# One read of the prompt heads' keys and queries instead of two, with the second half of the partitions written by the splitting engines

## The chip, the cores and the metric

The kernel runs on one core of a Trainium2 chip. The metric is the device time of one execution in microseconds (us); the time before is the median of three runs, 2407.51 us (2405.63 to 2414.55).

The core's engines each work through their own queue of instructions in order: PE (matrix multiply), DVE (vector), ACT (scalar), POOL (GpSimd), and SP, which here only issues DMA transfers. Sixteen DMA engines move the data.

## What is computed

The reference is one inference step of four layers over a prompt of 1024 tokens and a sample batch of 8 times 4 tokens. The change lies in layer 2, differential attention with 8 heads. Each head has two key halves and two query halves of 64 dimensions, one softmax for each, and one 128-wide value:

```python
q = rope_partial(q.reshape(bsz, t, 2 * N_HEADS, HEAD_DIM), pos) * (HEAD_DIM ** -0.5)
k = rope_partial(k.reshape(bsz, t, 2 * N_HEADS, HEAD_DIM), pos)
...
sc = jnp.einsum('bqhd,bkhd->bhqk', qi, k).astype(jnp.float32)
sc = jnp.where(kpos[None, :] <= qpos[:, None], sc, -jnp.inf)
w = diff_combine(jax.nn.softmax(sc, axis=-1), lam).astype(v.dtype)
return jnp.einsum('bhqk,bkhd->bqhd', w, v)
```

`diff_combine` is p1 - lam * p2 for the two halves of a head. The sample tokens attend to 2048 past positions each, through a paged cache of keys and values (`cache_k`, `cache_v`, 64 MB each).

## The kernel before, in words

Products are made with float32 operands split in two: a rounded high part in the type fp32r, and a low part (the value minus its high part). The projection stage `qkv` writes the rotated prompt keys and queries, transposed, to DRAM (`self.qkT`: 1024 rows of head dimension by 1024 tokens), because they don't fit on chip beside the rest.

`attn_layer` merges generators by costs: `qkv` and `zpath` run together with `sample_keys` (the pages of `cache_k`), then `heads` (the prompt heads) runs together with `sample_values` (the pages of `cache_v`). `self.ahead` is 1.1, so that the values end somewhat before the heads. Within this, the order of instructions on each engine is settled by the framework's planner, from its own estimate of each instruction's time; the heads' work has a raised priority.

`heads` goes through 64 blocks, 8 heads times 8 blocks of 128 queries. A block scores against the keys up to the diagonal (`score`), takes the exponent (`expo`, ACT), joins the two halves (`combine`, DVE), turns the weights (`turn`, PE and ACT), and applies them to the values (`apply`, PE). Scores for half s take one array in which both key parts lie across the partitions: `ks[h]` holds for half s the high part on 64 partitions (`own`) and the low part on the other 64 (`oth`). Queries `qhl` hold high and low part on both halves of the partitions, so that two matmuls over 128 partitions give all four products of the parts.

To fill these, `keys(h, g)` and `queries(h, g)` (g is a half of the tokens) are called 16 times each. `twice` (line 1179) allocates a raw tile and loads it with two transfers of SP (line 1183), each of 64 partitions and each carrying the whole 128 rows. ACT then rounds it (lines 1195 and 1203), and POOL subtracts (lines 1198 and 1204). Calls stand in the block loop: `queries(h, 1)` after block 1, `keys(h + 1, 0)` and `keys(h + 1, 1)` after blocks 4 and 5, `queries(h + 1, 0)` after block 6; the calls of head 0 are made while `zpath` still runs.

Raw tiles are a ring of two, shared with the weight loads of `load_w` (lines 110 to 112); `qhl` lies in a ring of two as well, shared with weights. The value pages come through a ring of five tiles (`vp`, line 1388), issued by SP, and are used by the matmuls `sacc` (line 1524). `cmask` (line 1327), which the first softmax needs, is loaded by SP too.

Of the kernel before, what the change touches and what calls it, by code (L numbers as in the profile page):

```python
# [10 lines left out]
F32 = mybir.dt.float32  # L11
# [4 lines left out]
ALU = mybir.AluOpType  # L16
# [30 lines left out]
class Trunk:  # L47
# [1123 lines left out]
    def heads(self, y):  # L1171
        nc = self.nc
        ident = self.ident
        lo_, hi_ = slice(0, 64), slice(64, 128)
        halves = ((lo_, hi_), (hi_, lo_))
        ks, V, sz, qs, O, ss = {}, {}, {}, {}, {}, {}


        def twice(q, h, g):
            t = self.raw([128, 2, 512], f"tok{q}{h}_{g}")  # L1180
            src = self.qkT[q][128 * h : 128 * h + 128, 512 * g : 512 * g + 512]
            for rows in halves[0]:
                nc.sync.dma_start(t[rows], src.rearrange("(s p) f -> p s f", p=64))
            return t

        def keys(h, g):
            if g == 0:
                ks[h] = self.ppa.tile([128, 2, T], F32R, tag="ks", bufs=self.n_ks, name=f"ks{h}")
                V[h] = self.ppa.tile([128, 8, 128], F32, tag="V", bufs=2, name=f"V{h}")
                nc.sync.dma_start(  # L1190
                    V[h], self.vd[:, 128 * h : 128 * h + 128].rearrange("(j p) f -> p j f", p=128)
                )
            t = twice(1, h, g)
            cs = slice(512 * g, 512 * g + 512)
            nc.scalar.copy(ks[h][:, :, cs], t)
            for s, (own, oth) in enumerate(halves):
                lo = ks[h][oth, s, cs]
                nc.gpsimd.tensor_tensor(lo, t[oth, s], lo.bitcast(F32), ALU.subtract)

        def queries(h, g):  # L1200
            t = twice(0, h, g)
            qhl = self.wtile([128, 2, 2, 512], F32R, f"qhl{h}_{g}")
            nc.scalar.copy(qhl[:, 0], t)
            nc.gpsimd.tensor_tensor(qhl[:, 1], t, qhl.bitcast(F32)[:, 0], ALU.subtract)
            qs[h, g] = qhl

        def product(st, h, qb, s, o, l0, w):
# [108 lines left out]
        def begin(h, qb):  # L1316
            return dict(h=h, qb=qb, S={}, P=[], rr=self.ropep.tile(
                [128, 20], F32, tag="rr", bufs=6, name=f"rr{h}_{qb}"))

        keys(0, 0)  # L1320
        queries(0, 0)
        keys(0, 1)
        yield 0

# [6 lines left out]
        for nxt in blocks[1:] + [None, None, None]:  # L1331
            if old:
                combine(old)
            if cur:
                h, qb = cur["h"], cur["qb"]
                expo(cur, 0)
                score(cur, 1)
                yield 220 * (qb + 1)
                if qb in (2, 5):
                    g = qb // 3  # L1340
                    sz[h, g] = self.pp.tile([128, 512], F32, tag="sz", bufs=self.n_sz, name=f"sz{h}_{g}")
                    nc.sync.dma_start(sz[h, g], self.zd[h][:, 512 * g : 512 * g + 512])
                if qb == 1:
                    queries(h, 1)
                    yield 430
                if h < 7 and qb in (4, 5):
                    keys(h + 1, qb - 4)
                    yield 430
                if h < 7 and qb == 6:
                    queries(h + 1, 0)  # L1350
                    yield 430
# [488 lines left out]
```

## Time and profile before

| what | value |
| --- | --- |
| median of three runs | 2407.51 us |
| profiled execution | 2409.33 us, its span 2407.7 us |
| PE busy over the span | 95% |
| DVE, ACT, POOL busy over the span | 60%, 39%, 14% |
| mean granted PE clock | 0.985 of full speed |
| the stretch in which heads and value pages run together | about 1490 to 1810 us |
| end of the heads | about 1845 us |

Line numbers are those of the kernel before. A row names the engine, the line, the operation, and the tile written and read (out<-in). "PEld" is PE's weight load, which runs beside its matmuls; "SPq" is a DMA being issued on SP. Idle time of an engine is put down to what ended it.

### The profile page before, as it was taken

How to read it: one execution, taken by the hardware profiler on the slowest of the kernel's cores; microseconds unless marked ns; L12 is line 12 of the kernel's file. 1: busy time of each engine (PE TensorE's matmuls, PEld its weight loads, DVE VectorE, ACT ScalarE, POOL GpSimd, SP SyncE). 2: the span in 40 equal slices, each digit the busy share in tenths (PEclk: the TensorE clock that was granted, in tenths of full speed). 3: DMA queues.
4: the chain of work that ended last, by engine and by line, in shares of the span. 5: the costliest groups of instructions: out<-in, count | busy, mean ns of one | idle time of the engine just before them, and what ended most of it. 6: DMA issues, size and time to landing. Idle time of an engine off the chain costs nothing.

```text
span 2407.7 us, 45325 instructions
## 1 busy us (share of the span) xinstructions
PE 2277.3 (95%) x17288; PEld 1946.8 (81%) x17288; DVE 1453.2 (60%) x3015; ACT 929.2 (39%) x1906; POOL 337.1 (14%) x541
## 2 busy tenths in 40 slices
PE   7999999999999999988999998888888999999997
PEld 4989999997888886766666886555557999999997
DVE  6865655457456545656555554677675477666555
ACT  4333333346544423322221113667665243333410
POOL 0200000001001000233223322333220000000000
PEclk9999999999999999999999998999999999999999
DMA  9243344423444535768677766999993222222442
GB/s 329 77 145 111 91 121 150 133 82 120 139 131 124 154 108 171 217 201 255 222 242 253 244 189 203 277 298 291 281 299 116 84 85 62 68 59 70 128 131 76
DMA packets 289391, 393.41 MB, mean 163 GB/s; under 512 B 18749, under 2 KB 197054, under 8 KB 289174
## 3 DMA queue, kind: packets, MB, share of 16 engines
q1 hardware_dynamic: 247190, 306.61, 42.1%
q0 software_dynamic: 20480, 67.13, 9.1%
q10 hardware_dynamic: 21504, 16.78, 2.1%
q8 instruction: 136, 2.23, 0.4%
q14 instruction: 81, 0.66, 0.1%
HBM read 331.14 MB, written 59.31 MB: 162 GB/s over the span
## 4 chain that ended last, share of the span: by engine, by line
PE 64%; issue 13%; DMA 11%; POOLq 5%; POOL 2%; DVE 2%; ACT 1%; SPq 1%; DVEq 0%; ACTq 0%
PE op L127 15%; PE inX L612 12%; PE inZ L612 6%; DMA vp<-cache_v 6%; PE xb L127 4%; PE z L127 4%; POOLq L1381 4%; PE in L127 3%; PE inY L612 3%; PE ada L200 3%; PE in L733 2%; PE in L648 2%; PE g L903 2%; POOL kp L1388 2%; PE sacc L1524 1%
## 5 line engine op out<-in xcount | busy, mean ns | idle before, releaser
L1099 PE MATMUL qk<-wq,ua 128*128 128x512 f32 x1152 | 284.1, 401 | 8.7 <-DVE wq L1067 5.5
L1099 PEld LDWEIGHTS qk<-wq,ua 128*128 128x128 f32 x1152 | 213.2, 189 | 68.4 <-DVE wq L1067 8.1
L1476 DVE STREAM_TRANSPOSE kt<-kp 128x512 f32<-128x512 f32 x256 | 172.0, 697 | 138.5 <-DMA kp<-cache_k 107.1
L1388 POOL DMA_DIRECT2D kp<-cache_k x256 | 137.9, 539 | 336.1 <-DVE kt L1476 188.8
L294 DVE SCALAR_TENSOR_TENSOR r<-op,gate,xr 128x384 f32<-128x384 f32 (+1 forms) x96 | 54.2, 570 | 127.4 <-PE op L127 82.5
L1262 ACT ACTIVATE P<-S,rr 128x512 f32<-128x512 f32 (+2 forms) x192 | 110.8, 583 | 47.1 <-DVE rr L1250 31.5
L1210 PE MATMUL S<-ks,qhl 128*128 128x512 f32 (+2 forms) x384 | 110.8, 395 | 13.8 <-ACT P L1262 7.4
L127 PE MATMUL zz<-ua,wz 128*128 128x384 f32 (+1 forms) x576 | 99.0, 331 | 7.0 <-DVE zt L1165 7.0
L1210 PEld LDWEIGHTS S<-ks,qhl 128*128 128x128 f32 x384 | 60.8, 196 | 54.8 <-ACT P L1262 30.7
L127 PEld LDWEIGHTS zz<-ua,wz 128*128 128x128 f32 x576 | 95.6, 193 | 11.4 <-DVE zt L1165 7.8
L127 PEld LDWEIGHTS z<-ub,wrz 128*128 128x128 f32 x576 | 92.6, 188 | 11.7 <-issue 10.1
L1524 PE MATMUL sacc<-vp,pv 128*16 128x256 f32 x1024 | 80.3, 389 | 22.9 <-DMA vp<-cache_v 22.7
L127 PE MATMUL z<-ub,wrz 128*128 128x384 f32 (+1 forms) x576 | 98.2, 326 | 0.0
L1303 PEld LDWEIGHTS pv<-V,wt 128*128 128x128 f32 x576 | 73.7, 194 | 22.5 <-ACT wt L1295 13.4
L127 PEld LDWEIGHTS xb<-ub,wrx 128*128 128x128 f32 x504 | 80.9, 188 | 12.7 <-issue 9.2
L1420 PE MATMUL sps<-kt,qbd 32*32 32x512 f32 x2048 | 78.8, 621 | 11.9 <-DVE kt L1476 11.9
L331 POOL TENSOR_TENSOR rs<-mv,mhalf 128x1 f32<-128x1 f32 (+1 forms) x36 | 19.1, 541 | 504.3 <-DVE mv L329 497.6
L127 PE MATMUL op<-ua,ub 128*128 128x384 f32 (+1 forms) x504 | 89.7, 333 | 0.0
L127 PEld LDWEIGHTS op<-ua,ub 128*128 128x128 f32 x504 | 81.9, 192 | 9.1 <-issue 9.0
L127 PE MATMUL xb<-ub,wrx 128*128 128x384 f32 (+1 forms) x504 | 87.9, 328 | 0.0
L1303 PE MATMUL pv<-V,wt 128*128 128x128 f32 x576 | 82.3, 284 | 5.8 <-ACT wt L1295 5.3
L200 PE MATMUL ada<-wada,ct 128*32 128x512 f32 x384 | 82.7, 616 | 4.1 <-DMA wada<-w_ada 2.9
(492 smaller groups left out, 5112.4 us busy)
## 6 DMA issues: line engine op xcount, KB each, us to landing
kp<-cache_k POOLq DMA_DIRECT2D x256, 256.0 KB, 3.8
vp<-cache_v SPq DMA_DIRECT2D x128, 512.0 KB, 10.0
wada<-w_ada SPq DMA_DIRECT2D x96, 512.0 KB, 4.2
xa<-xat SPq DMA_DIRECT2D x64, 192.0 KB, 2.6
wra<-a_w_in SPq DMA_DIRECT2D x24, 512.0 KB, 4.1
wrb<-a_w_in SPq DMA_DIRECT2D x24, 512.0 KB, 4.1
xr<-xa SPq DMA_DIRECT2D x64, 192.0 KB, 2.5
tok<-kd SPq DMA_DIRECT2D x32, 256.0 KB, 7.0
```

Source lines behind the costliest of these rows:

```text
L127: nc.tensor.matmul(ps[:, :n], wt[:, wp, k], self.ucols(units[k], up, c), start=i == 0, stop=i == 3 * KB - 1)
L200: nc.tensor.matmul(ps[c : c + 32, :], self.ct[:, k], wts[k // 2][:, k % 2], start=k < 4, stop=k >= 4, tile_position=(0, c),)
L612: nc.tensor.matmul(B[tgt][jj][:, :QH], w[n][:, wp, k], mov[k](jj, up), start=new and m == 0, stop=m == 11, skip_group_check=not new)
L1099: nc.tensor.matmul(ps, u[k][:, c0 : c0 + 128], wq[n, k // 2][:, wp, k % 2], start=i == 0, stop=i == 3 * KB - 1)
L1210: nc.tensor.matmul(st[:, o : o + w], qs[h, g][:, part, s, 128 * qj : 128 * qj + 128], ks[h][:, s, l0 : l0 + w], start=part == 0, stop=part ...
L1262: nc.scalar.activation(p[:, o : o + w], x["S"][s][i][:, :w], AF.Exp, scale=-1.0, bias=rr[:, 6 + s : 7 + s], accum_out=rr[:, c : c + 1])
L1303: nc.tensor.matmul(x["pv"], x["w"][kb // 4][:, j : j + 128], V[h][:, kb], start=kb == 0, stop=kb == qb)
L1381: ld, (r,) = nc.values_load_multi_w_load_instructions(self.ptab[0:1, idx : idx + 1], engines=[et], min_val=0, max_val=159)
L1388: d = eng.dma_start(t, a[src].rearrange(pat)[bass.ds(r, 1), :, cs].rearrange("a p f -> p (a f)"))
L1420: nc.tensor.matmul(ps[b][32 * g : 32 * g + 32, r], qf[rows, f, g, k], kt[rows, g, k], start=f == 0 and k == 0, stop=f == 1 and k == 3, til ...
L1476: nc.vector.transpose(ktv[:, :, j], ring.pop(0).rearrange("p (f t) -> p f t", t=32))
L1524: nc.tensor.matmul(acc[32 * g : 32 * g + 16, :], pt[:k, j, g], vv[:k, :, g], start=j == 0, stop=j == NPG, tile_position=(0, 32 * g))
```

## The change

`fetch` takes the place of `twice`: one transfer of 128 rows to 128 partitions, each row once, to a raw tile half as large. Partition p now holds row p, so half s of the head lies on its `own` partitions alone.

For keys, ACT rounds each half in an instruction of its own, in place on `own`, and POOL subtracts from `own` and writes the low part to `oth`. For queries, ACT rounds each half on `own`, DVE makes a second rounded copy on `oth`, and POOL subtracts twice, once into each half of the partitions.

```diff
-        def twice(q, h, g):
-            t = self.raw([128, 2, 512], f"tok{q}{h}_{g}")
-            src = self.qkT[q][128 * h : 128 * h + 128, 512 * g : 512 * g + 512]
-            for rows in halves[0]:
-                nc.sync.dma_start(t[rows], src.rearrange("(s p) f -> p s f", p=64))
+        def fetch(q, h, g):
+            t = self.raw([128, 512], f"tok{q}{h}_{g}")
+            nc.sync.dma_start(t, self.qkT[q][128 * h : 128 * h + 128, 512 * g : 512 * g + 512])
             return t
...
-            t = twice(1, h, g)
+            t = fetch(1, h, g)
             cs = slice(512 * g, 512 * g + 512)
-            nc.scalar.copy(ks[h][:, :, cs], t)
             for s, (own, oth) in enumerate(halves):
-                lo = ks[h][oth, s, cs]
-                nc.gpsimd.tensor_tensor(lo, t[oth, s], lo.bitcast(F32), ALU.subtract)
+                hi = ks[h][own, s, cs]
+                nc.scalar.copy(hi, t[own])
+                nc.gpsimd.tensor_tensor(ks[h][oth, s, cs], t[own], hi.bitcast(F32), ALU.subtract)
 
         def queries(h, g):
-            t = twice(0, h, g)
+            t = fetch(0, h, g)
             qhl = self.wtile([128, 2, 2, 512], F32R, f"qhl{h}_{g}")
-            nc.scalar.copy(qhl[:, 0], t)
-            nc.gpsimd.tensor_tensor(qhl[:, 1], t, qhl.bitcast(F32)[:, 0], ALU.subtract)
+            for s, (own, oth) in enumerate(halves):
+                hi = qhl[own, 0, s]
+                nc.scalar.copy(hi, t[own])
+                nc.vector.tensor_copy(qhl[oth, 0, s], t[own])
+                for rows in (own, oth):
+                    nc.gpsimd.tensor_tensor(qhl[rows, 1, s], t[own], hi.bitcast(F32), ALU.subtract)
             qs[h, g] = qhl
```

## Rows read from the trace of the kernel before

**Rows 1.** The page's slices: mean busy tenths of the DMA engines, 60 us each.

```profile
DMA  9243344423444535768677766999993222222442
```

**Rows 2.** Stretches of layer 2; columns in the first line, busy us with instruction counts.

```profile
core 0: us, PE busy (x) PEld busy (x) DVE busy (x) ACT busy (x) POOL busy (x), PEclk, DMA share, GB/s
1430.00:1490.00 60.00, 51.03 (x570) 45.33 (x568) 23.15 (x39) 13.64 (x21) 18.63 (x21) 0.94 0.50 137
1490.00:1810.00 320.00, 274.41 (x2262) 175.37 (x2262) 230.00 (x599) 215.01 (x663) 96.44 (x68) 0.97 1.01 291
1810.00:1850.00 40.00, 31.71 (x214) 26.00 (x207) 25.59 (x63) 24.53 (x67) 4.09 (x4) 0.96 0.22 70
```

**Rows 3.** DMA, 1490 to 1810 us: packets, then issues, size, median us to landing.

```profile
DMA packets 38182, 93.20 MB, mean 291 GB/s; under 512 B 3765, under 2 KB 12392, under 8 KB 38145
...
vp<-cache_v SPq DMA_DIRECT2D x128, 512.0 KB, 10.0
tok<-qd SPq DMA_DIRECT2D x28, 256.0 KB, 11.5
tok<-kd SPq DMA_DIRECT2D x24, 256.0 KB, 7.4
...
sz<-zd SPq DMA_DIRECT2D x14, 256.0 KB, 9.2
```

**Rows 4.** Waits of PE and PEld, 1490 to 1810 us: total us, times, longest.

```profile
PE sacc L1524 <- DMA vp<-cache_v: 22.7, 27, 1.9
PE wtp L1293 <- DVE P L1284: 7.1, 7, 1.8
PE S L1210 <- ACT P L1262: 6.3, 11, 1.6
...
PEld sacc L1524 <- DMA vp<-cache_v: 33.4, 34, 2.3
```

**Rows 5.** The tile tok, whole span: duration ns min/median/max, first and last start, form.

```profile
L1183 SPq DMA_DIRECT2D tok<-kd x32: 573/594/986, 1434.3 to 1749.3; - x32
L1198 POOL TENSOR_TENSOR ks<-tok,ks x32: 1261/1277/1682, 1440.6 to 1758.9; 64x512 fp32r<-64x512 f32 x32
...
L1195 ACT CAST ks<-tok x16: 1041/1046/1070, 1439.4 to 1756.4; 128x1024 fp32r<-128x1024 f32 x16
L1203 ACT CAST qhl<-tok x16: 1042/1045/1065, 1471.7 to 1786.9; 128x1024 fp32r<-128x1024 f32 x16
L1204 POOL TENSOR_TENSOR qhl<-tok,qhl x16: 2340/2364/2634, 1472.8 to 1788.0; 128x1024 fp32r<-128x1024 f32 x16
```

**Rows 6.** Nearest shapes elsewhere, by form: busy us, mean ns, idle before.

```profile
L1231 ACT CAST ua<-yt 128x512 fp32r<-128x512 f32 x16 | 9.9, 618 | 9.7 <-DVE yt L1229 9.7
...
L1413 DVE COPY qbd<-qsb 128x32 f32<-128x32 f32 x32 | 4.3, 166 | 0.5 <-PE spn L1429 0.5
...
L424 DVE TENSOR_TENSOR wsS<-wra,wsS 128x512 fp32r<-128x512 f32 x48 | 33.0, 690 | 5.0 <-ACT wsS L423 3.2
```

**Rows 7.** Timeline of POOL and DVE at two places: start, us, instruction.

```profile
1681.69 2.37 POOL L1204 TENSOR_TENSOR qhl<-tok,qhl 128x1024 fp32r<-128x1024 f32 x1 [4.55 <-ACT qhl L1203]
...
1681.82 2.93 DVE L1284 SCALAR_TENSOR_TENSOR P<-P,rr,P 128x640 f32<-128x640 f32 x1
...
1641.66 0.89 DVE L1284 SCALAR_TENSOR_TENSOR P<-P,rr,P 128x640 f32<-128x640 f32 x1
```

**Rows 8.** Waits of ACT for the raw tiles, 1490 to 1810 us.

```profile
ACT ks L1195 <- DMA tok<-kd: 7.8, 6, 2.9
...
ACT qhl L1203 <- DMA tok<-qd: 4.6, 3, 1.7
```

**Rows 9.** Timeline of POOL and SP at the start of the heads.

```profile
1472.85 2.40 POOL L1204 TENSOR_TENSOR qhl<-tok,qhl 128x1024 fp32r<-128x1024 f32 x1 [2.65 <-issue]
...
1475.27 1.23 SPq L1183 DMA_DIRECT2D tok<-kd  x2
...
1487.19 0.42 SPq L1327 DMA_DIRECT2D cmask<-cmask  x1
```

## The prediction

> **What bounds the kernel now.** PE is busy over most of the span, so the first question is where it is not, and whether the change lies there. I read the page's slices first. Beside the very first, the DMA digits stand at 9 in five slices only, the 26th to the 30th (1505 to 1806 us) [rows 1], and that is where the heads run beside the value pages. The table of stretches gives this stage as 1490 to 1810 us: DMA share 1.01 at 291 GB/s, PE busy 274.4 of 320 us, DVE 230.0, ACT 215.0, POOL 96.4; before it the DMA share is 0.50 and after it 0.22 [rows 2]. So in these 320 us the transfers are the fullest resource, and PE is idle for 45.6 us.
>
> The waits say what that idle time is for. PE itself waits 22.7 us, in 27 places, for a value page; its weight loads wait 33.4 us more, in 34 places, part of it while PE still has work [rows 4]. The waits for DVE (7.1) and for ACT (6.3) are next. So transfers set the pace, but by little at a time: 61 of 128 pages are late by 0.9 us on average (22.7 and 33.4 us over 61). The DMA list of the stage tells what shares the queue with them: 128 pages of 512 KB, and 52 transfers of keys and queries of 256 KB [rows 3], in 93.2 MB altogether. PE is what a saved microsecond must reach; behind the stage nothing waits for DMA to this degree, so time saved there should arrive at the end.
>
> **The change, part by part.** *Removed: half of the transfers.* Of the 52 in the stage 26 go, each 0.262 MB: 6.8 of 93.2 MB, 7.3%. At 291 GB/s that is 23.4 us of full DMA time. Were the stage nothing but DMA it would shrink by that; if all waiting of PE for pages went, by 22.7 us. Both are upper ends; the lower end is 0. In between: the five page tiles turn round in 5 times 320/128, 12.5 us, of which 10.0 is the transfer [rows 3]. With 7.3% less in the queue a page lands some 0.7 us sooner (estimate, 10.0 times 0.073). Lateness of 0.9 us falls by three quarters, and of PE's 22.7 us 17 go. I take -17, as both ends of the ring agree with it.
>
> *Removed: 32 issues on SP*, 26 of them in the stage, 0.59 us each [rows 5]. SP issues in order, and pages stand behind them. 26 calls put the next page forward by up to 0.6 us; most of these pages wait for a free tile anyway, so I take -1 (0 to -4).
>
> *ACT.* A cast of 128x1024 takes 1.05 us [rows 5]; the two of 64x512 that replace it are priced at 0.62 each, by the row of 128x512 [rows 6]. That is +0.19 us a call, 26 calls, 5 us on an engine that is 67% busy. PE's wait for the exponent is 6.3 us in the stage [rows 4]; I take +1 (0 to +3). For keys the first half is ready 0.4 us earlier.
>
> *DVE.* Two copies of 64x512 for each of the 13 to 14 query calls in the stage, 28. The trace has no such copy: the narrowest from SBUF takes 0.17 us, a two-input operation on 512 columns 0.69 [rows 6]. A copy reads one operand, so I take 0.45 in between: 13 us (5 to 19) on an engine that is 72% busy. These copies wait for the raw tile, and queued behind them are the minima, the joins and the page results that ACT and PE wait for. How long they may stand at the head of the queue is seen on ACT, which has that wait now: 4.6 us in 3 places for queries in the whole stage [rows 8], and the tile should land sooner. I take +2 (0 to +8).
>
> *POOL.* Keys keep two subtractions of 64x512, 1.28 us each; queries get four, 5.1 us, in place of one of 2.36 [rows 5]. That is +2.75 us a call, 38 us in the stage, and POOL goes from 30 to 42% busy. No row shows POOL writing to other partitions than it reads; I take the same 1.28, with 2.36 as the upper end, by which POOL would still stay under 70%. For latency it costs nothing: the score of half 0 needs the first two of the four, ready 0.62 + 2.55 = 3.2 us after landing, against 1.05 + 2.36 = 3.4 now; half 1 is due later.
>
> *POOL against DVE.* The subtraction for queries began at 1681.69 and took 2.37 us; a join on DVE (two SBUF inputs) that began 0.13 us later took 2.93 us, where the same shape takes 0.89 alone, and both ended within 0.7 us of each other [rows 7]. So DVE stands still until POOL's instruction is done. Chance of being caught grows with POOL's time, 5.1 against 2.36, but the mean delay falls with the length of one piece, half of 1.28 against half of 2.36 us; the product is 1.17 times the present one. I take +1 (0 to +5).
>
> [...]
>
> *The start of the heads.* The raw ring has two tiles, and its release hangs on POOL: SP issued a key fetch at 1475.27, when the subtraction of 1472.85 + 2.40 had just ended, and the mask that the first softmax needs left SP only at 1487.19 behind the later fetches [rows 9]. POOL's 2.75 us more come into this chain once or twice, less 0.6 us for each issue that is gone: +1 (-2 to +4).
>
> *The planner.* All durations that it estimates change, and so may the order on each queue. No row bounds this; a block is 320/58, 5.5 us, and I give it that much to both sides, 0 in the sum.
>
> **Sum.** -17 - 1 + 1 + 2 + 1 + 1 = -13 us. The profiled execution, 2409.33 us (1.6 of it outside its span of 2407.7), would go to 2396.3; it lies 1.8 us over the median of the runs, so against 2407.5 the forecast is 2394.5.
>
> **The rivals.** *The pages were late by little, and another wait takes over* (no change). For it: PE's idle time is 45.6 us, and only half is put down to pages; DVE and ACT are 72 and 67% busy, and catch up while PE waits. Against it: the DMA share of 1.01 is well above any of theirs. If two thirds of the 17 us turn into waits for the softmax, the sum is -2: 2405.5.
>
> *Transfers to 64 partitions cost more than their bytes* (faster than forecast). For it: a query fetch lands in 11.5 us, an `sz` of the same size on 128 partitions in 9.2. Against it: a key fetch lands in 7.4 [rows 3]. If a fetch now costs double its bytes, twice 23.4 us of DMA time goes, more than PE can collect: its whole 22.7 us of page waits, and SP's 4 us. With the +5 of the other terms the sum is -22: 2386.
>
> [...] The trace is undecided, with 11.5 and 7.4 us around 9.2.
>
> *DVE's copies get caught behind POOL* (slower). One mechanism: a copy comes to the head of DVE's queue after POOL has begun to subtract for the same tile, and stands until that piece ends, with the minima and joins behind it. Price: 28 copies held for up to 1.28 us each, 36 us, and 13 us of copying. For it: DVE is the fuller engine of the two that read the tile. Against it: the copy needs only the tile, as ACT's cast does, and may start 0.62 us before POOL can. It decides from the point where DVE lags by over 0.62 us behind ACT at most calls. If so, DVE's 230 us become 279, with little left of the shorter stage; if two thirds of the 49 us reach PE, the sum is -18 + 32 + 3 = +17: 2424.5.
>
> **How the numbers follow.** Forecast 0.52, another wait 0.23, more than bytes 0.10, copies caught 0.15. The range takes in the case of 2386, the planner's 5.5 us below it and some 2 us for the runs' own spread, and the second case with its upper ends, 2405.5 + 8; it leaves out the last case: 2378 to 2414. A measurement can tell about 0.5% from no change, 12 us, so 2395.5 is the line: three quarters of the forecast's chance, counting it with what a better planned order may add, and all of the third case lie under it, 0.49; above 2419.5 lies most of the last, 0.14; the rest is 0.37.
>
> **What would show it.** Right: 32 fetches of 256 KB, 86 MB or so in the stage, the stage near 305 us, PE's wait for pages under 10 us, POOL's query pieces four at 1.3 us. Wrong: PE's page waits halved but its waits for the join or the exponent grown by as much (second case); DVE copies of over 1 us, or DVE waits for `tok` over 5 us (last case); a DMA share that stays at 1.0 with a lower GB/s, by which the rate and not the amount was at fault; POOL pieces of 2 us and more when they write across the halves.

## The result and the profile after

The changed kernel takes 2426.93 us (median of six runs, 2424.38 to 2428.35), the kernel before, timed beside it, 2406.74: a ratio of 1.0073 [1.0047, 1.0099]. The forecast was 2394.5 with a range of 2378 to 2414, so it missed the time and the sign. One hundredth of the ratio is 24.1 us in all that follows.

The page of the changed kernel: the span, busy time by engine, the DMA slices, and the chain that ended last.

```profile
span 2423.6 us, 45378 instructions
PE 2295.1 (95%) x17288; PEld 1958.1 (81%) x17288; DVE 1488.1 (61%) x3047; ACT 940.8 (39%) x1938; POOL 390.2 (16%) x589
...
DMA  9243334424443445767777667877832221222342
...
PE 69%; issue 13%; DVE 5%; POOLq 5%; DMA 3%; ACT 2%; POOL 2%; SPq 0%; DVEq 0%; ACTq 0%
```

In the five slices that stood at 9 in [rows 1] now stand 8, 7, 7, 8 and 3: the transfers are no longer full. The stretches of [rows 2], now:

```profile
1430.00:1490.00 60.00, 54.21 (x535) 45.61 (x524) 33.01 (x69) 20.72 (x47) 26.81 (x29) 0.91 0.56 181
1490.00:1810.00 320.00, 275.78 (x2194) 174.58 (x2191) 246.74 (x577) 208.95 (x634) 137.59 (x106) 0.93 0.75 256
1810.00:1850.00 40.00, 31.20 (x178) 26.28 (x179) 28.51 (x78) 28.58 (x90) 4.10 (x4) 0.91 0.16 50
```

The DMA share fell from 1.01 to 0.75, and still PE did less in the same 320 us: 2194 matmuls against 2262, while its busy time went up, 275.8 against 274.4, at a granted clock of 0.93 against 0.97. DVE and POOL are fuller, 246.7 and 137.6 us against 230.0 and 96.4.

The DMA list of 1490 to 1810 us, to be read against [rows 3]:

```profile
DMA packets 32302, 82.05 MB, mean 256 GB/s; under 512 B 3088, under 2 KB 10827, under 8 KB 32265
...
vp<-cache_v SPq DMA_DIRECT2D x122, 512.0 KB, 5.1
tok<-qd SPq DMA_DIRECT2D x14, 256.0 KB, 5.4
...
tok<-kd SPq DMA_DIRECT2D x12, 256.0 KB, 3.8
```

The transfers of keys and queries are halved, and a page lands in 5.1 us where it took 10.0. What PE and its weight loads wait for, in the same stretch, against [rows 4]:

```profile
PE S L1213 <- ACT P L1265: 17.8, 13, 4.3
PE wtp L1296 <- DVE P L1287: 11.4, 8, 2.2
PE pv L1306 <- ACT wt L1298: 9.9, 10, 3.8
...
PEld S L1213 <- ACT P L1265: 35.3, 46, 4.6
```

No wait for a page is left (22.7 us before). Waits for the softmax stand in their place: for the exponent 17.8 us against 6.3, for the join 11.4 against 7.1, and for the turned weights 9.9 against 4.3. The tile `tok`, against [rows 5]:

```profile
L1207 POOL TENSOR_TENSOR qhl<-tok,qhl x64: 1258/1334/2018, 1461.3 to 1806.3; 64x512 fp32r<-64x512 f32 x64
L1196 ACT CAST ks<-tok x32: 604/617/627, 1433.2 to 1766.6; 64x512 fp32r<-64x512 f32 x32
L1197 POOL TENSOR_TENSOR ks<-tok,ks x32: 1259/1276/2142, 1433.9 to 1768.0; 64x512 fp32r<-64x512 f32 x32
...
L1205 DVE CAST qhl<-tok x32: 420/1164/1458, 1462.4 to 1805.2; 64x512 fp32r<-64x512 f32 x32
```

ACT's and POOL's pieces have nearly the durations that were priced (0.62 and 1.28 us). DVE's copy takes 0.42 us at the least and 1.16 at the median.

**Where the time went.** In the timelines the first score starts at 1482.8 us before and 1471.7 after, and the heads' last turned output ends at 1845.8 and 1862.1. From there to the end of the span it takes 562 us in both, so all of the loss stands at the end of the heads: 16.3 us, against 15.9 between the two profiled executions (2425.22 and 2409.33). The heads as one stretch, before, then after, in the columns of [rows 2]:

```profile
1482.80:1845.80 363.00, 307.99 (x2492) 203.50 (x2491) 252.95 (x658) 238.88 (x730) 104.68 (x77) 0.97 0.93 268
```

```profile
1471.70:1862.10 390.40, 328.74 (x2492) 217.30 (x2491) 288.16 (x688) 249.27 (x758) 153.09 (x122) 0.92 0.68 231
```

PE runs the same 2492 matmuls in both. The heads became 27.4 us longer: 20.7 of it is PE busy for longer with the same work, at a clock of 0.92 against 0.97, and 6.7 is PE idle (61.7 against 55.0 us). The loss is spread over the heads: by the starts of the last turned output of each, heads 2 to 7 took 43, 41, 47, 43, 41 and 42 us before and 42, 49, 52, 47, 50 and 49 after; the last one, during which no next head is fetched, took 39.5 and 38.8.

One place shows how it goes. The timeline of DVE, POOL, ACT and PE around 1623 us (start, us, instruction, idle time before it):

```profile
1623.24 1.04 POOL L1223 TENSOR_TENSOR O<-O,rsd 128x512 f32<-128x512 f32 x1
1623.25 2.73 DVE L1205 CAST qhl<-tok 64x512 fp32r<-64x512 f32 x2
...
1624.24 5.86 POOL L1207 TENSOR_TENSOR qhl<-tok,qhl 64x512 fp32r<-64x512 f32 x4
...
1627.17 1.81 DVE L1287 SCALAR_TENSOR_TENSOR P<-P,rr,P 128x512 f32<-128x512 f32 x1
...
1629.76 0.36 DVE L1253 CUSTOM_DVE_ANT_0 S<-S,cmask,rr 128x128 f32<-128x128 f32 x1 [0.17 <-DVE rr L1251]
...
1630.21 0.69 ACT L1265 ACTIVATE P<-S,rr 128x512 f32<-128x512 f32 x1 [4.23 <-DVE rr L1253]
...
1631.04 1.23 PE L1213 MATMUL S<-ks,qhl 128*128 128x256 f32 x3 [4.34 <-ACT P L1265]
```

The two copies start beside POOL's instructions and take 2.73 us instead of 0.84. The join behind them runs beside POOL's four pieces and takes 1.81 us, twice the 0.89 of a wider one in [rows 7]. The minimum that the next exponent needs (the scores are held with their sign turned) comes after both, ACT has stood for 4.23 us, and PE for 4.34. What the clock did there, in stretches of 5 us (columns as above):

```profile
1620.00:1625.00 5.00, 4.94 (x42) 2.73 (x40) 4.78 (x10) 4.38 (x16) 4.67 (x5) 1.00 0.97 298
1625.00:1630.00 5.00, 1.70 (x17) 1.12 (x9) 4.76 (x5) 0.92 (x4) 4.83 (x4) 0.99 0.90 357
1630.00:1635.00 5.00, 3.96 (x18) 3.34 (x22) 4.30 (x12) 3.76 (x12) 0.10 (x1) 0.50 0.19 55
1635.00:1640.00 5.00, 5.00 (x29) 3.23 (x22) 3.04 (x7) 0.75 (x3) 0.00 (x0) 0.50 0.53 158
```

PE was busy for 1.70 of 5 us; in the next 10 us it was granted 0.50, the lower of the two levels in the clock records of this trace (1.00 and 0.50). In the last row it is busy throughout and does 29 matmuls, in the first, at the full clock, 42 (not all of the same widths). So at this place a second loss follows the gap. In 17 of the 78 stretches of 5 us that cover the heads the granted clock is below 0.90, before in 6 of 72.

### The profile page after: what moved, and what is told of

Its sections match the earlier page's. It is cut to its first block, busy times and chain, and to the rows that moved or that the text cites. A ratio compares the mean times of both kernels' runs of the same rounds, so it can differ in the third digit from the quotient of the medians.

```text
span 2423.6 us, 45378 instructions
## 1 busy us (share of the span) xinstructions
PE 2295.1 (95%) x17288; PEld 1958.1 (81%) x17288; DVE 1488.1 (61%) x3047; ACT 940.8 (39%) x1938; POOL 390.2 (16%) x589
## 4 chain that ended last, share of the span: by engine, by line
PE 69%; issue 13%; DVE 5%; POOLq 5%; DMA 3%; ACT 2%; POOL 2%; SPq 0%; DVEq 0%; ACTq 0%
PE op L127 15%; PE inX L612 12%; PE inZ L612 6%; PE xb L127 4%; PE z L127 4%; PE in L127 4%; POOLq L1384 4%; PE inY L612 3%; PE ada L200 3%; PE S L1213 3%; PE pv L1306 2%; PE sacc L1527 2%; PE in L733 2%; PE in L648 2%; PE g L903 2%
## 5 line engine op out<-in xcount | busy, mean ns | idle before, releaser
L1213 PE MATMUL S<-ks,qhl 128*128 128x512 f32 (+2 forms) x384 | 116.4, 412 | 28.8 <-ACT P L1265 28.2
L1306 PEld LDWEIGHTS pv<-V,wt 128*128 128x128 f32 x576 | 80.7, 211 | 35.7 <-ACT wt L1298 21.1
L1207 POOL TENSOR_TENSOR qhl<-tok,qhl 64x512 fp32r<-64x512 f32 x64 | 87.7, 1370 | 96.9 <-ACT qhl L1204 93.6
L1306 PE MATMUL pv<-V,wt 128*128 128x128 f32 x576 | 89.6, 303 | 14.2 <-ACT wt L1298 11.8
L667 POOL COPY psv<-cp 128x32 f32<-128x32 f32 x14 | 7.3, 523 | 520.3 <-DVE cp L678 482.2
```

What stands on the lines that cost most here:

```text
L1207: nc.gpsimd.tensor_tensor(qhl[rows, 1, s], t[own], hi.bitcast(F32), ALU.subtract)
L1213: nc.tensor.matmul(st[:, o : o + w], qs[h, g][:, part, s, 128 * qj : 128 * qj + 128], ks[h][:, s, l0 : l0 + w], start=part == 0, stop=part ...
L1306: nc.tensor.matmul(x["pv"], x["w"][kb // 4][:, j : j + 128], V[h][:, kb], start=kb == 0, stop=kb == qb)
```

## The experiments

Two theories stood against each other at first. By the first, the relief of the transfers is worth what was forecast, and the narrow splitting work that pays for it (DVE's copies, POOL's pieces, or both) costs more than it. By the second, the relief itself does the harm: pages and heads that come sooner upset the order elsewhere. Line numbers below are those of each kernel.

**One read, and nothing else.** The single read, but every instruction of ACT and POOL in its old shape, reading the one tile twice. The rows of the other half are missing from the products. The edit is shown against the changed kernel, for the queries; the keys go the same way.

```diff
-            for s, (own, oth) in enumerate(halves):
-                hi = qhl[own, 0, s]
-                nc.scalar.copy(hi, t[own])
-                nc.vector.tensor_copy(qhl[oth, 0, s], t[own])
-                for rows in (own, oth):
-                    nc.gpsimd.tensor_tensor(qhl[rows, 1, s], t[own], hi.bitcast(F32), ALU.subtract)
+            tt = t.unsqueeze(1).to_broadcast([128, 2, 512])
+            nc.scalar.copy(qhl[:, 0], tt)
+            nc.gpsimd.tensor_tensor(qhl[:, 1], tt, qhl.bitcast(F32)[:, 0], ALU.subtract)
```

> The kernel before, with the single transfer of 128 rows for each call and nothing else changed: ACT's one cast and POOL's one or two subtractions keep their shapes of before, and both halves are taken from the same tile (so the rows of the other half are missing from the products; the work is the same). This is the removed transfers alone. Theory H (DVE's copies and POOL's longer subtractions hold the softmax chain up): the relief is a gain by itself, heads shorter by 15 to 25 us and the start some 10 us earlier, 2375 to 2392 us. Rival R (the relief itself turns into a loss: pages end early, and the heads are left alone with gaps and a lower clock): 2405 to 2425 us. Rival P (the planner's order, whatever the work): anywhere, with POOL and DVE waits as before.

Measured: 2387.77 us, 0.9913 [0.9888, 0.9937]. The heads as one stretch:

```profile
1472.20:1818.70 346.50, 309.18 (x2493) 205.00 (x2491) 251.75 (x658) 238.31 (x730) 104.53 (x76) 0.97 0.76 260
```

PE is idle for 37.3 us instead of 55.0, at the clock of before. PE's waits from 1490 to 1810 us:

```profile
PE S L1209 <- ACT P L1261: 15.7, 17, 2.1
PE wtp L1292 <- DVE P L1283: 7.3, 7, 1.8
PE pv L1302 <- ACT wt L1294: 3.8, 6, 1.2
```

No wait for a page is left here either, and the three waits for the softmax come to 26.8 us, against 17.7 before and 39.1 in the changed kernel. So the relief is worth 21 us (15 to 27), and the second theory falls: the one-read kernel also starts the heads at 1472.2 us, early as the changed kernel does, and ends them 27 us sooner than before. (Its profiled execution, 2381.89 us, was the fastest of its six, so what is read from it flatters the relief somewhat.)

**Keys only, and queries only.** The change for one of the two; the other is read twice as before. Both compute everything. The keys-only edit, against the changed kernel:

```diff
# keys only
         def queries(h, g):
-            t = fetch(0, h, g)
+            t = twice(0, h, g)
...
-            for s, (own, oth) in enumerate(halves):
...
+            nc.scalar.copy(qhl[:, 0], t)
+            nc.gpsimd.tensor_tensor(qhl[:, 1], t, qhl.bitcast(F32)[:, 0], ALU.subtract)
```

> The changed keys with the queries of before (two transfers, one cast, one subtraction). No DVE copies, POOL's time as before, half of the relief. Theory H: faster than before, by some half of the relief, 2388 to 2400 us. Rival R: half of the loss, 2410 to 2420 us. If POOL writing across the halves were dear: its pieces for keys over 1.4 us on average.

> The changed queries with the keys of before: DVE's copies and POOL's four pieces, half of the relief. Theory H: the loss stands here, and is larger than in the full change because less relief stands against it, 2425 to 2440 us. Rival R: half of the loss, 2410 to 2420 us.

Measured: keys only 2392.19 us, 0.9924 [0.9900, 0.9948]; queries only 2413.41 us, 1.0021 [1.0006, 1.0036]. PE's waits with keys only, 1490 to 1810 us:

```profile
PE S L1215 <- ACT P L1267: 16.6, 21, 3.0
PE sacc L1529 <- DMA vp<-cache_v: 9.0, 9, 2.1
```

Half of the key transfers less takes PE's page waits from 22.7 to 9.0 us. The keys' edit adds only ACT's two narrow casts; POOL's two pieces were there before, and now cross the partitions. It beats both kernels. With queries only no page wait is left in that stretch, but DVE's copies are drawn out as in the changed kernel (mean 0.98 us, 1.01 there), and the time goes the other way. The keys' time is what the first theory expected; the queries' time is below its 2425 to 2440 us and lies in the second's range, so the first theory has the cost of the queries' half too high. The halves don't add up: -0.76 and +0.21 hundredths make -0.55, where both together are +0.73.

**ACT in place of DVE.** The changed kernel, the second copy on ACT.

```diff
-                nc.vector.tensor_copy(qhl[oth, 0, s], t[own])
+                nc.scalar.copy(qhl[oth, 0, s], t[own])
```

> The full change with one exchange: the second rounded copy of the queries is made by ACT in place of DVE (32 casts of 0.62 us, 20 us more on ACT). Theory H with the copies as its main part: DVE is freed of 32 us (13 of copying, 19 of standing), 2400 to 2412 us. If POOL's longer subtractions against the joins are the main part: 2418 to 2430 us, and the joins stay long. Rival R: as the full change, 2420 to 2430 us.

Measured: 2409.34 us, 0.9994 [0.9980, 1.0009]; 19 us (12 to 26) of the changed kernel's time come back, though ACT goes to 238.6 us in the stage (209.0). PE's waits for `wt`, which ACT writes, are 12.9 us there (9.9), those for the join 8.1 (11.4), and PE is busy for 310.3 us in the heads instead of 328.7, at 0.96.

**The two kinds of narrow work, on the stage of before.** First POOL's four pieces alone, in place of its one subtraction of 128x1024; then DVE's copies alone, in place of half of ACT's cast. Transfers as before.

```diff
# four pieces
-            nc.gpsimd.tensor_tensor(qhl[:, 1], t, qhl.bitcast(F32)[:, 0], ALU.subtract)
+            for s in range(2):
+                for rows in halves[s]:
+                    nc.gpsimd.tensor_tensor(qhl[rows, 1, s], t[rows, s], qhl.bitcast(F32)[rows, 0, s], ALU.subtract)
# copies
-            nc.scalar.copy(qhl[:, 0], t)
+            for s, (own, oth) in enumerate(halves):
+                nc.scalar.copy(qhl[own, 0, s], t[own, s])
+                nc.vector.tensor_copy(qhl[oth, 0, s], t[oth, s])
```

> The kernel before, two transfers and all, with POOL's subtraction for the queries cut into four pieces of 64x512, each within its own partitions; nothing else. POOL gets 44 us more. If POOL's time against the joins matters by itself: 2415 to 2430 us. If it is covered as long as pages set the pace: 2405 to 2414 us. Pieces of 1.28 us, as those that cross the halves, would show that crossing costs nothing.

> The kernel before, two transfers and all, with DVE's two copies for each query call and ACT's two narrower casts in place of its wide one; POOL keeps its one wide subtraction. The same addition as e8 makes to e1, on a stage that the pages still pace. If pages cover DVE's added time (some 19 us): 2406 to 2413 us. If DVE's time reaches the end whatever paces the stage: 2420 to 2430 us.

Measured: pieces 2409.09 us, 1.0014 [0.9996, 1.0032]; copies 2418.75 us, 1.0039 [1.0018, 1.0060]. PE's waits for pages (1490 to 1810 us) with the pieces, then with the copies:

```profile
PE sacc L1526 <- DMA vp<-cache_v: 22.7, 28, 2.5
```

```profile
PE sacc L1526 <- DMA vp<-cache_v: 10.1, 10, 2.2
```

With the pieces POOL is busy for 155.1 us in the heads, 50 more than before, and the 64 joins take 71.7 us in place of 59.1, yet the time stands where it was, and PE waits for pages as before: the longer joins are covered. With DVE's copies PE waits less for pages, which fits a PE that is held up elsewhere, and the time is 9 us longer (4 to 14): between the two cases that were expected.

**The same two on the one-read kernel.** The same edits on top of the single read (products as there).

> The kernel with the single read alone (e1), and on top of it POOL's four pieces of 64x512 for the queries, as in the full change; ACT keeps its wide cast and DVE makes no copies. The products miss the rows of the other half, as in e1. Theory H1 (POOL's longer time against the joins is a large part of the loss): 12 to 25 us over e1, 2400 to 2412 us. Theory H2 (the copies on DVE are the loss, POOL's pieces alone cost little): within 6 us of e1, 2384 to 2394 us.

> The kernel with the single read alone (e1), and on top of it DVE's two copies for each query call and ACT's narrower casts, while POOL keeps its one wide subtraction. The products miss rows as in e1. If the copies cost by their own length (0.42 us each, 13 us on DVE): 3 to 10 us over e1, 2390 to 2398 us. If they stand behind POOL's one wide piece of 2.36 us as well: copies of 1 us and more, 10 to 20 us over e1, 2398 to 2408 us. If copies and four pieces are needed together for the loss: near e1, and e7 near e1 too.

Measured: with the pieces 2395.51 us, 0.9955 [0.9938, 0.9972]; with the copies 2404.61 us, 0.9991 [0.9974, 1.0008]. Against the one-read kernel that is +0.42 hundredths (0.12 to 0.72), 10 us, and +0.78 (0.48 to 1.08), 19 us; the bounds of a difference are the two intervals' half widths, added in squares. By the medians the same work costs more once the pages are on time. The intervals hold this up only just for the copies (0.39 hundredths more, 0.03 to 0.75) and not for the pieces (0.28 more, -0.07 to 0.63). The copies' durations with one read:

```profile
L1204 DVE CAST qhl<-tok x32: 419/422/1411, 1469.6 to 1785.8; 64x512 fp32r<-64x512 f32 x32
```

Seven of these took over 0.6 us, all 32 together 18.7 us, and they cost 19 us none the less: the time that was expected of copies of 1 us and more, without such copies. The pieces' time lies between the two that were expected.

**A copy that does not stand beside POOL.** The changed kernel, DVE's copy written as a maximum over an axis of one element; then the same on the one-read kernel with copies.

```diff
-                nc.vector.tensor_copy(qhl[oth, 0, s], t[own])
+                nc.vector.tensor_reduce(
+                    qhl[oth, 0, s], t[own].unsqueeze(2), axis=AX.X, op=ALU.max)
```

> [...]

> e8 with each DVE copy as a reduction over an axis of length one: 0.68 us each, 22 us on DVE, and never standing for POOL (e8: 13 us of copying and 5 of standing). The products miss rows as in e1. If DVE's added time reaches the end nearly one to one once the pages are no longer late: 16 to 24 us over e1, 2402 to 2411 us. [...]

Measured: 2414.05 us, 1.0028 [1.0010, 1.0046], 11 us less than the changed kernel (3 to 18); and 2396.59 us, 0.9956 [0.9943, 0.9968], 8 us less than with plain copies (3 to 14) and 10 more than the one-read kernel (4 to 17). The new form in the first of the two:

```profile
L1205 DVE TENSOR_REDUCE qhl<-tok x32: 679/680/682, 1467.5 to 1790.2; 64x512 fp32r<-64x512 f32 x32
```

It takes 0.68 us, and not one in 32 took longer, in a kernel with the POOL instructions of the changed kernel, where the copy took up to 1.46. In the one-read pair the reduction spends more of DVE's time (21.8 us against 18.7) and still gains, so DVE's busy time alone does not set the price; its time lies under the 2402 to 2411 us that were expected if DVE's added time reaches the end. What the copy costs beyond its own time on DVE can be that POOL or the join is held in turn, or only another planned order; the runs don't tell these apart.

**Copies ahead of POOL.** The changed kernel with the roles swapped: DVE rounds the own half, ACT makes the copy, and POOL's pieces, which come after both, subtract what DVE rounded.

```diff
+                nc.vector.tensor_copy(qhl[own, 0, s], t[own])
+                nc.scalar.copy(qhl[oth, 0, s], t[own])
+            for s, (own, oth) in enumerate(halves):
                 hi = qhl[own, 0, s]
-                nc.scalar.copy(hi, t[own])
-                nc.vector.tensor_copy(qhl[oth, 0, s], t[own])
```

> The full change with the two first copies exchanged and put ahead: DVE casts the queries' own half, from which POOL subtracts, and ACT makes the copy on the other half; both halves are cast before the first subtraction. Counts, shapes and values stay. POOL now waits for DVE's cast of the same tile, so that the cast can't stand behind its own tile's pieces. If standing is what the copies cost beyond their length: casts of 0.45 us on average instead of 1.0, DVE some 17 us freer, the time 8 to 14 us under the full change, 2411 to 2418 us. If the copies cost by being in DVE's queue at all, or POOL now starts later and holds the scores: 2422 to 2430 us.

Measured: 2423.19 us, 1.0059 [1.0042, 1.0075].

```profile
L1203 DVE CAST qhl<-tok x32: 407/426/1402, 1470.9 to 1799.7; 64x512 fp32r<-64x512 f32 x32
```

The median copy is no longer held, and DVE's total for them fell from 32.2 to 21.5 us. The time fell by 3 us, which the intervals don't tell from nothing (-11 to +4). POOL's idle time ahead of the pieces now ends with DVE's rounding (43.4 us, 5 times), where ACT's ended it in the changed kernel (93.6 us, 9 times). The time is the one that was expected if holding is not the matter. So less holding is not enough to bring the time back; as the swap also changes what POOL waits for, it doesn't tell what the holding costs by itself.

**The early start.** Only the six fetches of before the first score are single, in the kernel before; the scores made from those six miss the other half.

```diff
+            if h == 0 or (q == 1 and h == 1):
+                t = self.raw([128, 512], f"tok{q}{h}_{g}")
+                nc.sync.dma_start(t, src)
+                return t.unsqueeze(1).to_broadcast([128, 2, 512])
```

> The kernel before, in which only the six fetches that are made before the heads start (head 0's four, head 1's keys) are single transfers, in the form of e1; all other fetches are two transfers. The first head's products miss rows as in e1. If the earlier start of the heads comes from these six landing sooner: first score some 6 to 11 us earlier than in the kernel before, the heads as long as before, 2396 to 2403 us. If the earlier start comes from the planner's other order alone: it may show or not, without a relation to the six.

Measured: 2408.49 us, 0.9980 [0.9961, 0.9998], 5 us less than before (0.5 to 9), and the first score at 1483.9 us, against 1482.8. That start misleads, for this execution was late before it came to the edit: the matmuls `spt`, some 20 us ahead of the first fetch, start at 1414.7 us before, 1423.0 here, 1412.1 in the one-read kernel and 1412.0 in the changed one. From there to the first score, before and then here (columns of [rows 2]), and the wait of PE in it before that is gone here:

```profile
1414.65:1482.80 68.15, 62.76 (x626) 57.20 (x627) 29.78 (x53) 14.76 (x25) 17.71 (x23) 0.91 0.54 153
1423.02:1483.90 60.88, 60.86 (x626) 55.17 (x627) 29.43 (x52) 14.65 (x25) 18.26 (x23) 0.96 0.46 147
...
PE zz L127 <- DVE zt L1165: 5.4, 1, 5.4
```

The same matmuls take 68.1 us before and 60.9 here, 60.1 in the one-read kernel and 59.8 in the changed one. In all fourteen kernels it goes by the fetches: 67.7 to 69.0 us in the three that read everything twice, 63.5 and 63.9 with keys or queries only, 59.8 to 62.1 with single reads ahead of the heads. So the six single fetches do bring the first score nearer, by some 7 us, and the heads behind it are as long as before (362.3 us, 363.0). Another order of PE's queue is not the cause: up to a place behind the first score PE's matmuls stand in the same order before, here, in the one-read kernel and in the changed one. Behind it 61 of PE's 17288 matmuls are out of the old order in this kernel, 565 in the one-read kernel and 681 in the changed one (counted on the longest common sequence of tiles and shapes).

**All of them on one scale.** From one execution each: the heads from the first score to the last turned output, split by PE's busy time in that stretch, always for the same 2492 or 2493 matmuls; the mean granted clock; how many of the stretches of 5 us in it had one below 0.90; and how long PE was busy at the lower level, 0.50, by the clock records of the trace. Two of these executions are far from their kernel's median: the one-read kernel's was the fastest of six, that of `before, copies` the slowest of eight (2423.05 us).

| kernel | ratio | heads, us | PE busy | PE idle | clock | below 0.90 | busy at 0.50 |
| --- | --- | --- | --- | --- | --- | --- | --- |
| before | 1 | 363.0 | 308.0 | 55.0 | 0.97 | 6 | 18.8 |
| before, pieces | 1.0014 | 359.1 | 311.9 | 47.2 | 0.96 | 9 | 27.3 |
| before, copies | 1.0039 | 371.8 | 317.1 | 54.8 | 0.94 | 14 | 42.2 |
| before, six single | 0.9980 | 362.3 | 312.7 | 49.6 | 0.96 | 9 | 27.6 |
| one read | 0.9913 | 346.5 | 309.2 | 37.3 | 0.97 | 8 | 21.3 |
| one read, pieces | 0.9955 | 353.1 | 310.4 | 42.7 | 0.98 | 6 | 15.8 |
| one read, reductions | 0.9956 | 355.9 | 311.1 | 44.8 | 0.96 | 8 | 21.2 |
| one read, copies | 0.9991 | 363.9 | 311.9 | 52.0 | 0.96 | 10 | 23.5 |
| keys only | 0.9924 | 354.2 | 310.8 | 43.4 | 0.96 | 9 | 23.1 |
| queries only | 1.0021 | 371.3 | 315.6 | 55.8 | 0.94 | 14 | 34.1 |
| changed, ACT copies | 0.9994 | 370.5 | 310.3 | 60.2 | 0.96 | 8 | 24.7 |
| changed, reductions | 1.0028 | 373.8 | 316.3 | 57.5 | 0.95 | 12 | 28.5 |
| changed, swapped | 1.0059 | 378.0 | 319.1 | 58.9 | 0.94 | 14 | 38.1 |
| changed | 1.0073 | 390.4 | 328.7 | 61.7 | 0.92 | 17 | 55.9 |

On the one-read kernel the copies and the pieces show as idle time of PE (+14.7 and +5.4 us), in the changed kernel as idle time (+24.4) and as busy time at a lower clock (+19.5). How long PE is idle in all does not settle the clock: with ACT's copies it is idle for as long as in the changed kernel, and busy for 18 us less. The last column accounts for the busy time. In the changed kernel's trace the matmuls `wtp` of 128x128 started 213 ns apart at the median at the lower level and 109 at the full one. If PE works at half speed at the lower level, half of that column is lost time; with it taken off, PE's busy time is 296 to 303 us in all fourteen rows, though as it stands it runs from 308 to 329. By this the lower clock makes up some 18.5 of the 20.7 us by which PE is busy longer in the changed kernel than before. No run changed the clock by itself, so this is read from one execution each, and not shown by a run. Over the whole execution its mean was 0.977 to 0.979 in each of the six runs of the changed kernel, and 0.982 to 0.987 in the six of the one-read kernel.

## Why the prediction was wrong

The sum had savings of 18 us and costs of 5. The runs have savings of 21 us (15 to 27) and costs of 39 (30 to 47, the changed kernel over the one-read kernel). So the savings held, and the costs failed.

**The bound was right, and the savings came out nearly right, in part by luck.** PE's page waits went, all 22.7 us, and in the profiled executions PE is idle for 17.7 us less in the heads of the one-read kernel, against the term of -17. But the step to that term was wrong: a page was to land 0.7 us sooner and landed 5 us sooner, so all of the page waits went and not three quarters of them. Two things that the term does not have then brought the number near. Waits for the softmax took 9.1 us back (17.7 to 26.8, from 1490 to 1810 us): the second rival's mechanism is real, and takes less than half. And 5.9 us of the idle time of before is one wait for `zt` at the start of the heads, which is gone as well in the kernel with six single fetches.

**The third case's price came true, hidden under the loss.** It held, at a chance of 0.10, that transfers to 64 partitions cost more than their bytes. In the heads the sixteen DMA engines were busy for 338 us before (0.93 of 363.0) and 263 in the one-read kernel (0.76 of 346.5): 75 us less, where the bytes that went are worth 24 at the rate of before. The packet records of the traces say where. Packets of 2 KB, the size of one row of these transfers, took 141 ns at the median before and 84 with the single read; 2120 of 8960 took under 90 ns before, 5083 of 5503 with the single read. Packets of the pages (4 KB) went from 165 to 159 ns. The 2 KB packets alone took 46 us less of the sixteen engines' time, twice the 23.4 of the sum, as the case had it, though no row of before gave its factor of two. Its time of 2386 and the one-read kernel's 2387.77 are near each other partly by chance, as the case counted 5 us of costs that the one-read kernel doesn't have. Whether it is the 64 partitions or the order of the rows in these transfers that costs, no run tells.

**DVE is the step that failed.** "I take +2 (0 to +8)" for the copies. Their own price was right, 0.42 us free against 0.45. On the one-read kernel they cost 19 us (12 to 26), and 9 (4 to 14) where pages were still late. The step set 13 us against an engine "72% busy" and took the idle 28% for room. What the sum lacked is a wait: DVE's work lies in a chain of score, minimum, exponent, join and turn, and a copy at the head of DVE's queue delays that chain when the chain is what PE waits for. With the pages on time it is: the three longest waits of PE in the changed kernel are all for the softmax, 39.1 us from 1490 to 1810 us. Given to ACT, the copies' 19 us come back (12 to 26). That the delay runs through this chain is seen at 1623 us and in these waits; no run shows it apart from the copies' holding and the planned order.

**POOL was mis-sized in the same way.** The pieces take the 1.28 us that was assumed, 1.27 in place and 1.27 to 1.33 across the halves. "For latency it costs nothing", and +1 (0 to +5) against DVE: nothing measurable on the stage of before (0.14 hundredths, -0.04 to 0.32), but 10 us (3 to 17) on the one-read kernel. The 64 joins take 59.1 us before and 71.7 with the pieces, 63.5 with one read and 71.6 with its pieces. The likeliest cover on the stage of before is the pages' lateness, the very thing that the change takes away; the two costs are not far enough apart to show it.

**The last rival's time came true, its mechanism in part.** It gave 2424.5 against 2426.93, at a chance of 0.15, and the sign set for it, copies of over 1 us, appeared. No row of the kernel before shows that POOL holds a copy. In the changed kernel's trace each of the 23 copies of over 0.43 us began while a two-input instruction of POOL ran, and ended 0.28 or 0.29 us after it. Copies were held: 32.2 us for the 32, 18.8 more than 0.42 each, half of the 36 that it priced. What spoke against it, that a copy could start 0.62 us ahead of POOL, did not hold: at 1623.25 us the copies met another POOL instruction, and then the pieces. A form that took 0.68 us in all 32 places gave 11 us back; a swap that took away more than half of the holding gave nothing that can be told; and copies that were hardly held cost 19 us on the one-read kernel. So being caught is a part of the loss and not the whole, and the nearness of the two times is partly chance.

**A term was missing.** The sum prices each microsecond of PE's waiting once. In the changed kernel PE has nine gaps of over 2 us in the heads, each followed by a stretch at the lower clock, as at 1625 us; before there was one, in the one-read kernel two. 20.7 of the heads' 27.4 us are PE busy longer with the same matmuls, and the lower clock makes up some 18.5 of these. But the swapped kernel has two such gaps and 38.1 us at the lower level, so whether idle time brings the clock down, and which, is left open. [Rows 2] had the granted clock at 0.97 with 45 us of idle time; no step asked what clock would be granted after a longer gap.

**The start had the wrong sign.** +1 was taken; the first score came 11 us sooner in the changed kernel, as in the one-read kernel, and POOL's longer pieces did not keep it from that. 8 of the 11 us lie between `spt` and the first score, and the six single fetches by themselves give 7 there. The step counted 0.6 us for an issue that is gone, and not what waits for the tiles to land. The other 3 us stand ahead of the first fetch, where the executions differ by more than that whatever the kernel (1412 to 1423 us). In the changed kernel the gain was down to 2 us by the end of the fourth head (1677 us, before 1679).

**ACT and SP.** The casts take 0.617 us as priced. Their cost was not tried apart: the keys-only kernel has the keys' casts, and stands 0.11 hundredths (within 0.34) above the one-read kernel, which has none but halves the query transfers too. SP's saving was not tried apart either.

**What stays open.** Copies and pieces cost 0.78 and 0.42 hundredths each on the one-read kernel, and the changed kernel stands 1.60 above it; the excess of 0.40 has an uncertainty of 0.43, so the two costs may simply add up. The two halves of the change, with -0.76 and +0.21, do miss their joint +0.73 by 1.28, with an uncertainty of 0.38. In the table the misfit of 28 us in the heads lies on both sides: PE's busy time (+2.8 and +7.6 apart, +20.7 together) has 10 us of it, its idle time (-11.6 and +0.8, +6.7) 17. The clock and the planned order are both candidates: any edit but that of the six fetches puts 541 to 688 of PE's matmuls out of the old order, and no run held that order fixed.

## What to carry to other kernels

Price the work that a change adds on the stage as it will be once the change has removed its bound: the idle shares of the other engines, and covers such as late transfers, are partly made by that bound and can go with it. Here the medians say so (copies 9 and 19 us, pieces 3 and 10), though the intervals leave it open for the pieces. Where a change has parts that save and parts that pay, run each part alone; here the keys' half alone is 2392.19 us and beats both kernels, because it halves its transfers without giving DVE or POOL an instruction more. An engine that is busy for 70% and takes part in every round of a chain, as DVE at 72% here, may have no room in the other 30%: ask what stands behind the new instruction in its queue. And read a stretch from a place ahead of the edit to one behind it, rather than one start time alone: an execution can be late before it comes to the edit.

## What the runs showed of the hardware

- A float32 copy of 64x512 on DVE took 0.42 us alone and, in the changed kernel, up to 1.46 beside POOL's two-input subtraction; the same copy written as a reduction over one element took 0.68 in all 32 places, in a kernel with the same POOL work.
- POOL writing to the other half of the partitions than it reads took what it takes in place: 1.272 us in place at the median, 1.276 across for keys, 1.268 across for queries when no copy on DVE ran beside it.
- Packets of 2 KB took 141 ns at the median while transfers of 256 KB to 64 partitions were among them, and 84 ns when all went to 128 partitions; the pages' packets of 4 KB took 165 and 159.
- A page of 512 KB landed in 5.1 us at a DMA share of 0.75 and in 10.0 at 1.01, with 82.1 and 93.2 MB in the stage: the share fell by a quarter, the bytes by 12%.
- At one place PE, at full clock, was busy for 1.70 of 5 us and was granted 0.50, the lower level, in the 10 us after. PE's busy time for the same matmuls differed by up to 21 us between kernels, and by under 7 once half of its time at the lower level was taken off.
